# A rotation by 180 degrees: the last load in two transfers, and the first store issued only when the first of them has landed

## Chip, cores and metric

One core of a Trainium2 chip. The metric is device microseconds (us) of one execution; lower is better. Unless a line says otherwise, a time is the median of the runs of one session, and all runs compared here were at a granted clock of 1.0. A ratio is the mean time of one kernel's fast runs over that of the other's of the same rounds, so it is not quite the ratio of the medians beside it.

## The reference

```python
def setup_inputs():
    batch, c, h, w = 32, 3, 256, 256
    return {"x": np.random.randn(batch, c, h, w).astype(np.float32)}

def reference(x):
    return np.rot90(x, k=2, axes=(-2, -1)).astype(np.float32)
```

Each of the 96 images of 65,536 floats is reversed end to end: 25.17 MB in, 25.17 MB out.

## The kernel before

An image is cut into 4 rows of 16,384 floats, so 32 images fill 128 partitions of 64 KB each. Three tiles A, Bt and Ct hold all images. VectorE reverses each row in place, by swapping mirrored blocks of 2,048 floats through a scratch tile T; the store reverses the order of an image's 4 rows by its access pattern.

```python
    G = 32
    E = L // 4          # 16384
    J = E // 8          # 2048
    # ... views x4 (loads) and o4 (stores), tiles A, Bt, Ct, T: cut ...
    def load(t, g):
        nc.sync.dma_start(out=t[:, :], in_=x4[g])

    def store(t, g):
        nc.sync.dma_start(out=o4[g][:, ::-1, :], in_=t[:, :])

    def inside(t):      # 12 copies of 128 x 2048
        for lo in range(0, E // 2, J):
            hi = E - lo - J
            copy(T[:, :], back(t, hi, hi + J))
            copy(t[:, hi:hi + J], back(t, lo, lo + J))
            copy(t[:, lo:lo + J], T[:, :])

    load(A, 0)
    load(Bt, 1)
    load(Ct, 2)
    for g, t in enumerate((A, Bt, Ct)):
        inside(t)
        store(t, g)
```

All six transfers are issued by SP (SyncE) on one queue. So they pass through the 16 DMA engines in the order of issue: load A, load B, load C, store A, store B, store C.

## Time and profile before

| | before |
|---|---|
| median | 123.0 us (122.93 to 123.27, 3 runs) |
| span of the profiled run | 121.2 us |
| share of the span in which DMA engines hold packets | 97.4% |
| VectorE busy | 44.2 us, 36% |
| bytes moved | 50.33 MB |

The page, the timeline and the windows are read in the prediction below. One more view belongs to the argument: who waited for whom (columns: engine, line and tile that waited, what it waited for, us in total, times, longest).

```profile
DVE T L52 <- DMA Ct<-in_x_dram: 5.4, 1, 5.4
DVE T L52 <- DMA Bt<-in_x_dram: 4.3, 1, 4.3
```

VectorE does the same work on B and on C, and the loads are of equal size, but it waits 1.1 us longer for C. VectorE is not the bound, so that wait costs nothing by itself. It is a gauge: load C comes 1.1 us later than the rhythm of the loads would have it.

### The profile page before, as it was taken

What the parts mean: (1) busy time and instruction counts of PE and PEld (TensorE: products, weight loads), DVE (VectorE), ACT (ScalarE), POOL (GpSimd) and SP (SyncE); (2) the same over time, 40 slices, a digit from 0 to 9 for tenths busy, and PEclk for the clock granted to TensorE, in tenths of its full rate; (3) what the DMA queues carried; (4) which work ended last, traced back from release to release, by engine and by line L of the source; (5) the groups of instructions that cost most, each with busy time, mean ns of one, the idle gap of its engine ahead of it and who ended that gap; (6) DMA issues with size and microseconds to landing.
All of it is one profiled execution on the core that took longest, in us unless ns stands there. A gap on an engine that the chain in (4) does not pass through costs nothing.

```text
span 121.2 us, 91 instructions
## 1 busy us (share of the span) xinstructions
DVE 44.2 (36%) x36; POOL 0.2 (0%) x4
## 2 busy tenths in 40 slices
DVE  0000000599994199998039999500000000000000
POOL 0000000000000000000000000000000000000000
DMA  9779977997799879978989977997799779977980
GB/s 346 346 346 411 627 346 346 454 584 346 346 454 584 346 346 498 541 346 346 346 346 584 454 346 346 606 433 346 346 606 433 346 346 627 411 346 346 671 368 0
DMA packets 864, 50.33 MB, mean 415 GB/s; under 512 B 96, under 2 KB 96, under 8 KB 96
## 3 DMA queue, kind: packets, MB, share of 16 engines
q1 hardware_dynamic: 864, 50.33, 97.4%
HBM read 25.17 MB, written 25.17 MB: 415 GB/s over the span
## 4 chain that ended last, share of the span: by engine, by line
DMA 34%; DVE 25%; another core or an unknown queue 4%; issue 1%; SPq 0%; DVEq 0%
DMA Bt<-in_x_dram 34%; DVE T L52 8%; DVE Bt L52 8%; DVE Ct L52 8%; SPq L55 0%; DVEq L52 0%
## 5 line engine op out<-in xcount | busy, mean ns | idle before, releaser
L52 DVE COPY T<-A 128x2048 f32<-128x2048 f32 x4 | 4.9, 1227 | 22.7 <-DMA A<-in_x_dram 22.6
L52 DVE COPY T<-Ct 128x2048 f32<-128x2048 f32 x4 | 4.9, 1228 | 5.5 <-DMA Ct<-in_x_dram 5.4
L52 DVE COPY T<-Bt 128x2048 f32<-128x2048 f32 x4 | 4.9, 1227 | 4.4 <-DMA Bt<-in_x_dram 4.3
L52 DVE COPY A<-T 128x2048 f32<-128x2048 f32 x4 | 4.9, 1227 | 0.1
L52 DVE COPY Bt<-T 128x2048 f32<-128x2048 f32 x4 | 4.9, 1227 | 0.1
L52 DVE COPY Bt<-Bt 128x2048 f32<-128x2048 f32 x4 | 4.9, 1227 | 0.1
L52 DVE COPY Ct<-T 128x2048 f32<-128x2048 f32 x4 | 4.9, 1227 | 0.1
L52 DVE COPY A<-A 128x2048 f32<-128x2048 f32 x4 | 4.9, 1226 | 0.1
L52 DVE COPY Ct<-Ct 128x2048 f32<-128x2048 f32 x4 | 4.9, 1226 | 0.1
L87 POOL MEMSET const-bfloat16-1.0<- 128x1 bf16 x1 | 0.1, 102 | 0.0
L87 POOL MEMSET const-uint8-127<- 128x1 uint8 x1 | 0.1, 102 | 0.0
L87 POOL MEMSET const-float32-1.0<- 128x1 f32 x1 | 0.1, 99 | 0.0
L87 POOL MEMSET const-float32-0.0<- 128x1 f32 x1 | 0.1, 98 | 0.2 <-issue 0.2
## 6 DMA issues: line engine op xcount, KB each, us to landing
A<-in_x_dram SPq DMA_DIRECT2D x1, 21.8
Bt<-in_x_dram SPq DMA_DIRECT2D x1, 40.7
Ct<-in_x_dram SPq DMA_DIRECT2D x1, 60.7
out_dram<-A SPq DMA_DIRECT2D x1, 44.1
out_dram<-Bt SPq DMA_DIRECT2D x1, 44.0
out_dram<-Ct SPq DMA_DIRECT2D x1, 42.8
```

Source lines behind the costliest of these rows:

```text
L52: tc.keep_in_program_order(nc.vector.tensor_copy(out=dst, in_=src))
L87: nc = _bacc.Bacc("TRN2", target_bir_lowering=False, num_devices=1)
```

## The change

The intent is to keep the first store out of the DMA queue until the loads are nearly through, without paying for a wait with idle engines. The store is held back by a dependency (the *gate*) on most of the last load (the *body*, 58 KB of each row), and the remaining 6 KB of each row (the *tail*) keep the engines busy while the store is issued. The place where the queue goes over from loads to stores is called a *turn* below.

```diff
-    def load(t, g):
-        nc.sync.dma_start(out=t[:, :], in_=x4[g])
+    def load(t, g, lo, hi):
+        return nc.sync.dma_start(out=t[:, lo:hi], in_=x4[g][:, lo:hi])
 ...
-    load(A, 0)
-    load(Bt, 1)
-    load(Ct, 2)
-    for g, t in enumerate((A, Bt, Ct)):
+    TAIL = 1536
+    load(A, 0, 0, E)
+    load(Bt, 1, 0, E)
+    body = load(Ct, 2, 0, E - TAIL)
+    load(Ct, 2, E - TAIL, E)
+    inside(A)
+    first = store(A, 0)
+    tc.add_manual_dep(
+        first.ins, body.ins.name,
+        mybir.DependencyInfo(mybir.DependencyClass.Sync, mybir.DependencyReason.DATA),
+        reason="the first store is queued while the last strip is on its way")
+    for g, t in ((1, Bt), (2, Ct)):
         inside(t)
         store(t, g)
```

More of the change, by code (lines that the diff above doesn't have):

```diff
@@ L52, in copy @@
         tc.keep_in_program_order(nc.vector.tensor_copy(out=dst, in_=src))
-    def load(t, g):
-        nc.sync.dma_start(out=t[:, :], in_=x4[g])
+    def load(t, g, lo, hi):
+        return nc.sync.dma_start(out=t[:, lo:hi], in_=x4[g][:, lo:hi])
     def store(t, g):
-        nc.sync.dma_start(out=o4[g][:, ::-1, :], in_=t[:, :])
+        return nc.sync.dma_start(out=o4[g][:, ::-1, :], in_=t[:, :])
     def inside(t):
```

## The prediction

> **What bounds the kernel now.** I read the page first: the share of each engine, the DMA lines and the issues.
>
> ```profile
> DVE 44.2 (36%) x36; POOL 0.2 (0%) x4
> ...
> q1 hardware_dynamic: 864, 50.33, 97.4%
> HBM read 25.17 MB, written 25.17 MB: 415 GB/s over the span
> ...
> A<-in_x_dram SPq DMA_DIRECT2D x1, 21.8
> Bt<-in_x_dram SPq DMA_DIRECT2D x1, 40.7
> Ct<-in_x_dram SPq DMA_DIRECT2D x1, 60.7
> out_dram<-A SPq DMA_DIRECT2D x1, 44.1
> out_dram<-Bt SPq DMA_DIRECT2D x1, 44.0
> out_dram<-Ct SPq DMA_DIRECT2D x1, 42.8
> ```
>
> The 16 DMA engines hold packets during 97.4% of the span and VectorE works 36% of it, so the DMA engines are the bound, and the one VectorE chain matters only if a store is not queued when its turn comes. The last column of an issue is the time from issue to landing, most of which is standing in line behind the earlier transfers on the one queue.
>
> Next I asked the timeline when the transfers were issued, so that landings can be worked out.
>
> ```profile
> 0.73 0.39 SPq L55 DMA_DIRECT2D A<-in_x_dram  x1
> 1.18 0.42 SPq L55 DMA_DIRECT2D Bt<-in_x_dram  x1
> 1.64 0.43 SPq L55 DMA_DIRECT2D Ct<-in_x_dram  x1
> ...
> 37.70 0.63 SPq L58 DMA_DIRECT2D out_dram<-A  x1
> ...
> 57.11 0.55 SPq L58 DMA_DIRECT2D out_dram<-Bt  x1
> ...
> 77.58 0.54 SPq L58 DMA_DIRECT2D out_dram<-Ct  x1
> ```
>
> Issue plus time to landing gives landings at 22.5, 41.9, 62.3, 81.8, 101.1 and 120.4 us. The differences are 19.4, **20.4**, 19.5, 19.3 and 19.3: all transfers are equal in bytes, and one, the last load, takes about 1.1 us longer. Every store is queued long before its turn: A at 37.70 for 62, B at 57.11 for 82, C at 77.58 for 101. Then I looked at the moment in question, with windows as long as a packet (columns: stretch, its length, busy VectorE and GpSimd, clock, DMA share, GB/s).
>
> ```profile
> 55.60:58.00 2.40, 1.45 (x2) 0.00 (x0) 1.00 1.01 410
> 58.00:60.40 2.40, 0.00 (x0) 0.00 (x0) 1.00 1.29 382
> 60.40:62.80 2.40, 0.35 (x1) 0.00 (x0) 1.00 1.01 437
> 62.80:65.20 2.40, 2.33 (x3) 0.00 (x0) 1.00 1.01 437
> ```
>
> The rate dips and the packets' summed time rises (1.29 is more than all engines' time, because a packet is booked whole in the window where it starts). So packets that start at 58 to 60 are longer. The trace's records of single DMA packets say the same. Chained end to start, they give 16 engines of 48 packets of 65,536 bytes, 24 loads and then 24 stores:
>
> ```
> packet of each engine   starts (us)     ends (us)       length (us)   mean excess over 2.418
> 1st (first load)        1.74..2.40      4.84..5.30      2.63..3.46    0.72
> 2nd to 23rd                                             2.42..2.43    0.00
> 24th (last load)        57.98..58.44    61.42..62.06    3.17..3.86    1.13
> 25th (first store)      61.42..62.07    63.84..64.48    2.42          0.00
> 26th to 48th                            ..120.02        2.42          0.00
> ```
>
> The sum closes: a mean start of about 1.9, 48 x 2.418 = 116.1, 0.72 and 1.13 give 119.8, inside the spread of last ends, 119.38 to 120.02. **Apart from start and end, the only time not spent at line rate is 1.1 us where loads turn into stores.** That is all that this change can win.
>
> **What the Trainium skill says.** "DMA: Bandwidth & Descriptors", section "Where 436 GB/s comes from", puts the ceiling of the 16 ports at 435 GB/s. The trace agrees: 16 x 65,536 bytes in 2.418 us is 434 GB/s, the windows show 437, for loads and stores alike. Nothing is left inside the transfers. The same page, "Two DMAs through the same engine are not ordered", says that descriptors of one queue start in order but are pipelined, with separate queues for an engine's read and write sides. The trace fits: there is no gap between one load and the next, nor between stores. It follows, as my inference, that an engine can begin to read the first store's tile while the last load is still being written. The same page, "Latency and other measured facts", gives about 600 ns to the first byte for a transfer issued from SP. Here the first issue ends at 0.73 + 0.39 = 1.12 and the first packet starts at 1.74: 0.62, in agreement; the last of the engines starts 0.66 later. "SBUF — State Buffer", section "SBUF: two separate sides", says that compute and DMA do not share ports. Packets are 2.42 us with VectorE busy (at 30 us) and idle (at 90 us), so I give the 12 copies of 1.23 us per tile no part in this.
>
> **The change part by part.**
>
> (1) The last load is cut. Engine by engine, 8 packets of 65,536 bytes become 8 of 59,392 and 8 of 6,144. At the same bytes per us these are 2.418 x 58/64 = 2.191 and 0.227 us. The body takes 17.53 us from the start at 41.06 to 41.53, so its last data is there at 58.59 to 59.06; the tail would end 1.81 us later, at 60.40 to 60.87. One more issue of about 0.43 us falls near 2 us, where SP has nothing else to do: nothing on the path. Overhead of the eight small packets is not measured in this trace; I allow 0 to 0.3 us.
>
> (2) The first store waits. A landing is seen 0.32 to 0.37 us after an engine's last packet (22.21 to 22.57, 41.54 to 41.91, 62.07 to 62.39 in the records and VectorE's starts). SP may thus issue store A at 59.06 + 0.35 = 59.4 instead of 37.70. The issue takes 0.63 us, then 0.62 to the first packet: 60.65, and 0.66 more for the last engine, 61.3. The tail keeps the engines busy to 60.40 to 60.87, so they would idle some 0.3 us. Without the tail the wait would be naked, with 1.9 us of idleness; this is what the tail is for. Store B, ready at 57.08, now goes right after A, at about 60.1, still 20 us early.
>
> (3) What the 1.13 us becomes. It is inside the load's own last packet and delays the load's landing, while the first store shows nothing. I take it for the store's reads running into the last load. With no store in the ring, the tail should run at line rate. In return the first store starts cold and may have to fill, as the first load did (0.72 us mean excess; the last engine, which sets the end, only 0.22). I choose 0.2 to 0.6 for reading SBUF.
>
> Sum for the latest engine: the first store starts at 61.3, plus 0.4 of fill, against 62.07 today: -0.4 us. All later packets are 2.418 as before, so the end moves by the same amount.
>
> (4) VectorE waits for two landings of C instead of one, some hundredths of a us, and starts near 61.3 instead of 62.45. Store C is issued near 76.5 where it is needed at 100. Worth nothing either way.
>
> **The rivals.**
>
> *R1: the turn costs its 1.1 us whatever is queued*, for instance because reads from HBM must drain before the engine reads SBUF. For it: there is just one turn in the trace and it is the one slow place. Against it: the lateness lies in the load, not in the store. Then the tail's last packets stretch to 61.5 to 62.0, the store's late arrival at 60.65 to 61.3 hides in that, and the time stays at 122.9 to 123.2.
>
> *R2: the new wait costs more than it saves.* SP's wait for the body, issue and first packet is 1.9 us against a tail of 1.81, so any extra delay is idle time of all engines. If the store's fill is the first load's 0.72 and its issue is slow by another 0.5, the loss is 0.72 + 0.5 + 0.3 = 1.5 against 1.13 saved: 123.4.
>
> *R3: the whole 1.13 comes back*, because the store's descriptors arrive just in time and fill costs nothing: 122.0. For it: store packets show no excess anywhere. Against it: the arrival sum above is 0.3 us late before any fill.
>
> *R4: VectorE or a late store becomes the bound.* Against it: 20 us of slack for stores B and C, as worked out above. I give it nothing.
>
> **Range and chances.** The step from the median of 123.0 is my own mechanism's -0.4, so 122.6. R3 sets the favourable end, 122.0, and R2 the other, 123.4; the three runs of before span 0.34 us, so I widen slightly below: 121.9 to 123.4. To be faster by over 2% the change would have to win 2.46 us, more than twice what the turn costs; slower by over 2% needs 2.46 us of added idleness, a naked wait of 1.9 plus a full fill, with nothing won. I give each 0.01.
>
> **What would show each step.** In the changed trace the tail's landing minus B's landing shows the stretch: 19.4 us if it is gone, 20.4 if R1 holds. The issue of store A should stand at 59.4. Its landing minus the tail's landing shows idleness and fill: 19.3 plus 0.4 to 1.0. Store B and C should follow at 19.3 each. In the packet records, the eight small packets should last 0.23 us, with a gap of 0 to 0.6 us before the first store's packet, which is itself 2.4 to 3.0. The prediction would be wrong if the small packets were much dearer than their bytes, if the split load lost line rate all along its 58 KB packets, or if store packets written after the gate ran slower than 2.418.

## The result

The changed kernel takes 122.14 us (122.01 to 122.36, 5 runs) against 123.04 us (122.93 to 123.27, 5 runs): a ratio of 0.9928, 95% interval 0.9916 to 0.9941. That is 0.9 us, clear of noise and under 2%. The profiled spans went from 121.2 to 120.2 us.

The page of the changed kernel, DMA lines and issues (the last number of an issue is us to landing):

```profile
q1 hardware_dynamic: 1008, 50.33, 97.3%
HBM read 25.17 MB, written 25.17 MB: 419 GB/s over the span
...
Ct<-in_x_dram SPq DMA_DIRECT2D x1, 7424.0 KB, 57.7
Ct<-in_x_dram SPq DMA_DIRECT2D x1, 768.0 KB, 59.2
A<-in_x_dram SPq DMA_DIRECT2D x1, 21.8
Bt<-in_x_dram SPq DMA_DIRECT2D x1, 40.7
out_dram<-A SPq DMA_DIRECT2D x1, 21.3
```

The same bytes took 144 packets more (128 data packets of 6 KB and 16 for one more completion), and the rate over the span rose from 415 to 419 GB/s. Store A lands 21.3 us after its issue instead of 44.1. Its timeline and that of the other stores:

```profile
59.48 0.63 SPq L58 DMA_DIRECT2D out_dram<-A  x1
60.20 0.55 SPq L58 DMA_DIRECT2D out_dram<-Bt  x1
...
76.51 0.54 SPq L58 DMA_DIRECT2D out_dram<-Ct  x1
```

Store A went from 37.70 to 59.48, store C came 1.1 us earlier. The waits, against the two lines shown of before:

```profile
DVE T L52 <- DMA Ct<-in_x_dram: 4.4, 1, 4.4
DVE T L52 <- DMA Bt<-in_x_dram: 4.3, 1, 4.3
```

The gauge reads 0.1 us instead of 1.1: VectorE waits nearly as long for C as for B. So the slow place at the end of the loads is gone. The trace's records of single DMA packets, by the 16 engines, show it directly, with what came in its place (idle is the stretch of 57 to 64 us less the summed length of the packets in it):

```
                                before              after
last load data ends (us)        61.42..62.06        60.33..60.84
last 64 KB load packet          3.17..3.86          none (58 KB: 2.19, 6 KB: 0.23)
first store packet starts       61.42..62.07        60.76..60.94
first store packet, length      2.42                2.47..2.48
mean idle of an engine, 57..64  0.00                0.16
mean period of the packets of
  stores B and C                2.4147              2.4209
last store packet ends          119.38..120.02      118.90..119.11
```

The last engine now starts its stores 1.13 us earlier (60.94 for 62.07). It gives back 0.06 us in the first store packet and 0.0062 us in each of 24 store packets, which makes 0.15. The rest, 0.92, is the end's move from 120.02 to 119.11.

### The profile page after: what moved, and what is told of

Read it like the earlier page. It is cut to its first block, busy times and chain, and to the rows that moved or that the text cites. A ratio compares the mean times of both kernels' runs of the same rounds, so it can differ in the third digit from the quotient of the medians.

```text
span 120.2 us, 93 instructions
## 1 busy us (share of the span) xinstructions
DVE 44.2 (37%) x36; POOL 0.2 (0%) x4
## 4 chain that ended last, share of the span: by engine, by line
DMA 34%; DVE 25%; another core or an unknown queue 4%; issue 1%; SPq 0%; DVEq 0%
DMA Bt<-in_x_dram 34%; DVE T L52 8%; DVE Bt L52 8%; DVE Ct L52 8%; SPq L55 0%; DVEq L52 0%
## 6 DMA issues: line engine op xcount, KB each, us to landing
Ct<-in_x_dram SPq DMA_DIRECT2D x1, 7424.0 KB, 57.7
Ct<-in_x_dram SPq DMA_DIRECT2D x1, 768.0 KB, 59.2
out_dram<-A SPq DMA_DIRECT2D x1, 21.3
```

## The experiments

The theory: a store queued behind the last load is read ahead by the DMA engines, and this costs the load's last packets 1.1 us; the gate removes it and the tail hides the gate. The rivals: that the cutting of the load does it; that any turn from loads to stores costs as much; that the change of the written memory, not of the read one, costs it. Twelve runs tell these apart. All except the last gave the right result. What is said of packets comes from the one profiled run of each kernel; each time is compared with the kernel before in the same session. "In the ring" below is the issue's start plus 1.28 us, as measured from issue to first packet in the changed kernel (59.48 to 60.76).

### Only the cut, no gate

```diff
-    first = store(A, 0)
-    tc.add_manual_dep(first.ins, body.ins.name, ...)
+    store(A, 0)          # as early as before; the load stays cut in 58 + 6 KB
```

> The last load cut into 58 KB and 6 KB as in the change, but the first store issued as early as before (about 37.7 us). Theory (the store's reads, queued behind the load, run into the end of the load; the gate alone removes that): the tail lands about 20.4 us after B, the first store follows with no gap, 123.0 us. Rival (cutting the last load into small pieces is what removes the slow packet): tail lands 19.4 us after B and the time is near the changed kernel's 122.1 us.

Measured: 123.32 us against 122.99, ratio 1.0018 (1.0004 to 1.0031). The page's issues of this run:

```profile
Ct<-in_x_dram SPq DMA_DIRECT2D x1, 7424.0 KB, 58.0
Ct<-in_x_dram SPq DMA_DIRECT2D x1, 768.0 KB, 60.8
```

The tail is issued 0.47 us after the body in both kernels, so it lands 3.3 us after the body here, and only 2.0 us after it in the changed kernel (57.7 and 59.2). By the packet records, an engine's eight 6 KB packets take 3.13 us in the mean, 1.26 more than at the 0.234 of the changed kernel, and the excess is in the first five of them: the disturbance is whole, only spread over smaller packets. The cut without the gate is worth nothing; it costs 0.2%.

### Only a gate, no cut

```diff
     body = load(Ct, 2, 0, E)         # whole
     first = store(A, 0)              # depends on body
```

> The last load whole, the first store issued only when it has landed. Theory: the last load's packets all take 2.42 us (load C lands 19.4 us after B, near 61.2), then a naked wait: issue near 61.2, first store packet 1.25 us later, so engines idle 1.6 to 2.1 us; the store phase begins near 62.5, about 1.7 us later than in the changed kernel and 0.4 us later than before: 123.4 to 123.9 us. Rival (the turn from loads to stores costs 1.1 us by itself, whatever is queued): load C's last packets still take 3.5 us, and the time is above 124.5 us.

Measured: 122.52 us, ratio 0.9961 (0.9949 to 0.9973). This missed both expectations, and the reason was in the timeline: the scheduler let the second store, which had no such dependency, go first.

```profile
57.60 0.63 SPq L58 DMA_DIRECT2D out_dram<-Bt  x1
61.98 0.55 SPq L58 DMA_DIRECT2D out_dram<-A  x1
```

So this was not a naked wait. It became the first point of a series: a store in the ring at 58.9 us cost the last load packet 0.23 us on average, not 1.13. I repeated the run with both stores held back:

> The last load whole; both the first and the second store held back until it has landed, in the order A, B (in e2 the second store slipped ahead of the first at 57.6 us, so that run was not a naked wait). Theory: last load packets all 2.42 us, landing of C near 61.2, issue of store A near 61.2, first store packet 1.28 us after the issue, near 62.5: the store phase begins 1.4 us later than with timed gate 1 (60.9), 123.4 to 123.9 us. Rival (a turn costs 1.1 us of its own): the last load packets or the first store packet are 1 us longer, 124.5 us or more.

Measured: 123.92 us against 122.94, ratio 1.0074 (1.0041 to 1.0106). Windows of that run (stretch, its length, VectorE, GpSimd, clock, DMA share, GB/s) and its first issue:

```profile
58.00:60.40 2.40, 0.00 (x0) 0.00 (x0) 1.00 0.95 410
60.40:62.80 2.40, 1.40 (x2) 0.00 (x0) 1.00 1.03 437
62.80:65.20 2.40, 2.33 (x3) 0.00 (x0) 1.00 0.69 300
```

```profile
61.37 0.63 SPq L58 DMA_DIRECT2D out_dram<-A  x1
```

The share of over 1 in the stretch 58.0 to 60.4 of the kernel before is gone: all 24 load packets take 2.42 us (the third window's low rate is the hole seen through late booking, since a packet counts where it starts). The first store packet comes 1.27 us after the issue, at 62.64, and is 2.46 to 2.48 us long. The turn from loads to stores thus has next to no price of its own in this run (0.05 us in the first store packet); the engines just stand idle for 2.04 us on average. That is what the tail hides in the changed kernel, where 0.16 us of idleness are left. A gate without a tail loses.

### The moment of entry alone

Here the load is whole, and the store is held back by one or two extra VectorE copies after tile B's twelve, that is by time and not by a landing.

```diff
+    for _ in range(n):               # n = 1, 2
+        late = nc.vector.tensor_copy(out=T[:, :], in_=back(Bt, 0, J))
     first = store(A, 0)              # depends on the last of them
```

> The last load whole, and the first store held back not by a landing but by one extra VectorE copy after tile B's twelve (end near 58.3 us), so its packets should reach the engines near 59.6 us, 0.8 to 1.3 us before the last load packets would end at 60.4 to 60.9. Theory: part of the stretch comes back, last packets 2.4 to 3.6 us, time between 122.1 and 123.0. If the stretch needs only that a store is in the ring at any moment before the load's end, it is whole (3.55 us mean) and the time is 123.0. Rival (the split matters): 123.0 or more.

> As the run before with two extra VectorE copies (end near 59.6 us), so that store A is issued at the moment it is in the changed kernel, without any split of the load. Theory (the moment at which the store enters is all that counts): last load packets 2.42 us, first store packets near 60.9, 122.1 to 122.2 us, the same as the changed kernel. Rival (the split or the small packets do it): last packets 3.5 us and 123 us or more.

Measured: 122.0 us, ratio 0.9922 (0.991 to 0.9935), and 122.23 us, ratio 0.9941 (0.9929 to 0.9953). Both last load packets are undisturbed (means 2.436 and 2.439), and the time is that of the changed kernel without any cut. The second is as expected within noise; the first missed, for a part of the stretch was to come back: a store in the ring 0.7 to 1.2 us before the load's end does next to no harm (0.02 us). Its issue:

```profile
58.45 0.63 SPq L58 DMA_DIRECT2D out_dram<-A  x1
```

To find where the harm begins, the store was tied to the twelfth and to the eleventh copy of tile B itself:

```diff
+    first = store(A, 0)              # depends on copy number 12 (11) of inside(Bt)
```

> The last load whole, the first store held back until the twelfth and last copy of tile B (issue near 57.1, in the ring near 58.4, 2.0 to 2.5 us before the load's end without disturbance). e2, with a store in the ring at 58.9, showed 0.2 us of excess in the last load packet; timed gate 1, at 59.7, none. If the disturbance comes only when the store is there before the read side has finished the load, the excess here is between 0.2 and 0.8 us, 122.2 to 122.6 us. Rival (time in the ring does not matter once the store is there before the load's end): 1.1 us and 123.0.

> As the run before, held back until the eleventh copy of tile B (issue near 55.9, in the ring near 57.1, 3.3 to 3.8 us before the load's end, while the last but one packet of each engine is moved). If what counts is being there before the read side turns, the excess is whole, 0.9 to 1.2 us, 122.9 to 123.1 us. If the excess grows with the number of load packets that the store waits behind (as many as 9 in the kernel before), it is about 0.3 us and the time 122.3.

Measured: 122.3 us, ratio 0.9965 (0.9916 to 1.0013), and 123.06 us, ratio 1.0002 (0.9969 to 1.0035). The time of the first is not clear of noise (one of its four runs took 123.28), so the reading rests on its packets. The issue of the twelfth-copy run, then that of the eleventh-copy run with its window (to be held against 1.29 and 382 of before):

```profile
57.48 0.63 SPq L61 DMA_DIRECT2D out_dram<-A  x1
```

```profile
55.96 0.63 SPq L61 DMA_DIRECT2D out_dram<-A  x1
```

```profile
58.00:60.40 2.40, 0.00 (x0) 0.00 (x0) 1.00 1.18 355
```

Together, with mean excess of the last 64 KB load packet over 2.418 us:

```
first store in the ring at (us)   excess (us)   median time (us)
about 39    (before)              1.13          123.0
57.2        (eleventh copy)       1.10          123.06
58.8        (twelfth copy)        0.30          122.3
58.9        (store B slipped in)  0.23          122.52
59.7        (one extra copy)      0.02          122.0
60.9        (two extra copies)    0.02          122.23
62.65       (naked gate)          0.00          123.92
```

The times come from three sessions. It makes next to no difference whether the store stands in line for 22 us or for 4. The price falls from whole to a quarter between 57.2 and 58.8 us, while the last load packets start being recorded at 57.9 to 58.9. Past that, lateness brings idleness. I read it as the moment when an engine's read side has finished the loads; the trace has no record of the read side by itself, so this is an inference. Engine by engine it is not seen: in the twelfth-copy run the excess is 0.45 us for the packet that starts first, at 57.91, 0.73 for one at 58.32, 0.02 for one at 58.37 and 0.09 for the last, at 58.80.

### A longer tail

```diff
-    TAIL = 1536
+    TAIL = 2048
```

> The changed kernel with a tail of 2048 elements (8 KB of each row) instead of 1536. The body lands about 0.6 us earlier, so store A is issued near 58.85 and is in the ring near 60.1, 0.3 to 0.8 us before the tail's end. By timed gate 1 this is late enough for no disturbance and early enough for no idle time: the first store packets start right behind the tail, the time 121.9 to 122.1 us, 0.1 to 0.2 us under the changed kernel. If the disturbance starts as soon as the store is in the ring, up to 0.5 us slower instead.

Measured: 122.11 us, ratio 0.993 (0.9902 to 0.9959); issue at 59.08, mean idleness of an engine 0.035 us instead of 0.16. The tail is undisturbed. The tenth of a us that could be won is within noise of the changed kernel's 122.14: these two tails cannot be told apart, and others were not tried.

### How much store is needed for the harm

With timed gate 1 for the bulk, a strip of each row of tile A is stored early and waits behind the loads.

```diff
+    nc.sync.dma_start(out=o4[0][:, ::-1, :n], in_=A[:, :n])   # n = 128, 1024: early
     ...
+    first = nc.sync.dma_start(out=o4[0][:, ::-1, n:], in_=A[:, n:])   # depends on the extra copy
```

> As timed gate 1, but 512 bytes of each row of tile A (8 packets, 4 KB per engine) are stored early, queued behind the last load from about 37.8 us on, while the other 65,024 bytes of each row wait for the timed gate. If the lost 1.13 us is the store's reading ahead by bytes (at 27 bytes per ns it would be 31 KB per engine), 4 KB cost 0.15 us in the last load packet. If it is the price of any turn of the read side while loads are on the way, it is whole, about 1.1 us, in the last load packet. In both cases the gated rest follows at line rate; the time is 122.2 (bytes) or 123.1 us (any turn), plus some tenths for small packets.

> The same with 4 KB of each row early (8 packets, 32 KB per engine), the rest gated. Reading ahead by bytes: 32 KB are as much as the 31 KB above, so the whole 1.1 us. Any turn: also 1.1 us. With s1 this tells whether the cost grows with the bytes queued: s1 at 0.15 and this at 1.1 means bytes, both at 1.1 means the turn, both near 0 means that neither is right.

Measured: 122.01 us, ratio 0.9925 (0.991 to 0.9939), and 122.97 us, ratio 1.0002 (0.9986 to 1.0019). The last load packet's excess is 0.03 us with 4 KB per engine queued and 0.89 us with 32 KB, against 1.13 with the whole tile. (The strips were issued at 26.5 us, when the block they need was ready, not at 37.8; both are long before the moment that counts.) A turn to SBUF that is queued early is almost free when little follows, so the price is not for the turn; it grows with the bytes that are queued, from 4 KB to 32 KB by 0.86 us and from there to the whole tile by 0.24. At 27.1 bytes per ns (65,536 in 2.418 us), 0.89 us is the time of 24 thousand bytes and 1.13 us that of 31 thousand. The numbers were 0.15 and 1.1 in my sum, so bytes is the better theory, though not an exact one.

### Two turns in one program

```diff
     load(A), load(Bt)
-    load(Ct)
     store(A)
+    load(Ct)             # behind store A in the queue; then store(Bt), store(Ct)
```

Load C also depends on the last copy of tile A here, so that the scheduler leaves it behind store A; the stores have no gate.

> The same six transfers with the third load queued behind the first store: load A, load B, store A, load C, store B, store C, no gate anywhere. There are two turns from loads to stores and one from stores to loads. If each turn from loads to a queued store costs 1.1 us, the last packets of loads B and C take 3.5 us each, and the total is at least 1.1 us above the kernel before: 124.1 us if the turn from stores to loads is free, up to 125.2 if it costs as much. Rival (the loss is a single effect of the first store of the program, a cold start of the store path): load C's last packet is 2.42 us and the time is 123.0 to 123.3.

Measured: 122.92 us against 122.95, ratio 1.0005 (0.9982 to 1.0027). The windows around the two turns, load B to store A and load C to store B, and the issue of store B:

```profile
38.60:41.00 2.40, 0.00 (x0) 0.00 (x0) 1.00 1.42 437
...
77.80:80.20 2.40, 0.00 (x0) 0.00 (x0) 1.00 1.05 437
```

```profile
58.04 0.55 SPq L61 DMA_DIRECT2D out_dram<-Bt  x1
```

At the first turn the last load packet takes 3.29 to 3.48 us (mean excess 0.99), at the second 2.42 to 2.69 (mean 0.10), although store B had been in the queue for about 20 us. The turn from stores back to loads in between is clean, 2.418 on both sides. **My theory of a price at each such turn falls here; in this run, the only one with two turns, the price is paid once.** The rival, an effect of the first store of the program, was right in this, though not as a cold start of the store path: the naked gate's first store is just as cold and pays 0.05 us. What fits these runs is an inference: when the engines first come to a tile in SBUF with enough of it queued, their reading gains a lead over their writing of 24 to 31 thousand bytes, at the expense of the load that is still being written; a lead once gained is kept, so the second turn is nearly free. One small finding points the same way: in five runs where the store entered late (the changed kernel, both timed gates, the naked gate, the longer tail) the later store packets follow each other in 2.4205 to 2.4209 us, in all others in 2.4147 to 2.4151. But it does not follow the price: the run with 4 KB stored early, which paid 0.03 us, is at 2.4151, and the copy within HBM below, whose last load packet is clean, at 2.4147. No run here shows the lead itself.

### The written memory or the read one

In place of store A, a copy from HBM to HBM of the same size is queued behind the last load.

```diff
+    nc.sync.dma_start(out=o4[0][:, ::-1, :], in_=x4[0])
     inside(A)
-    store(A, 0)
```

> Wrong result on purpose: in place of the first store, a copy of the same size from HBM to HBM is queued right behind the last load (first third of the result comes out unreversed); then stores B and C. If the loss comes from the read side's change from HBM to SBUF, the 24th packet of each engine (last load) now takes 2.42 us, and the 1.1 us appear in the 32nd, the last of the HBM to HBM copy, just before store B begins to read SBUF. If it comes from the write side's change from SBUF to HBM, it stays in the 24th or 25th and the 32nd is clean. The copy's own packets may be slower than 2.42 us.

Measured: one run of 128.25 us, its state unknown, so that nothing is read from its time; the result is wrong, as intended (relative error 0.82). The window that was slow in the kernel before:

```profile
58.00:60.40 2.40, 0.00 (x0) 0.00 (x0) 1.00 0.95 410
```

The last load packet takes 2.426 us, with 64 KB packets that write HBM queued behind it since 2 us. So the change of the written memory from SBUF to HBM is not enough to cause it; in the runs here the price appears only where what follows reads from SBUF. No run has a transfer behind the load that reads SBUF without writing HBM, so it stays open whether reading from SBUF is enough alone. The second half of the expectation, 1.1 us in the 32nd packet, can't be judged: the copy's own packets, from the second on, take 2.76 to 4.25 us, and its last, at a mean of 3.51, does not stand out.

## Why the prediction was right, and where its sum was off

- **The bound and the size of the prize** held. The only slow place of the stream was the 1.13 us at the end of the loads, and no version's median got under 122.0 us. That the time fell inside the range says little, for the range ran from a gain of 1.1 us to a loss of 0.4; the forecast's own step, to 122.6, had less than half of the gain.
- **The mechanism of the gate** held: the small packets and 58 KB packets took 0.234 and 2.19 us (0.227 and 2.191 predicted), the body's data was there at 58.46 to 58.99 (58.59 to 59.06), SP issued store A at 59.48 (59.4), the first engine started it at 60.76 (60.65). Stores B and C had slack, VectorE's earlier start on C was worth nothing.
- **The step that was mis-sized is (3), with the end of (2)**: "the first store starts at 61.3, plus 0.4 of fill". Both numbers leaned on the program's first load. There the engines start over a spread of 0.66 us; store A's start over 0.18, so the last engine starts at 60.94 and not 61.3. And a cold store has next to no fill: 0.06 us, and 0.05 in the naked gate. Together 0.7 us better than the sum.
- **One cost was not in the sum**: the store packets follow each other 0.0062 us later than before, 0.15 us in all. The prediction had named store packets slower than 2.418 us as a sign of being wrong, and in this small measure it came: they are 2.424 long in the mean of stores B and C. The sum's -0.4 is -0.37 unrounded (61.3 + 0.4 - 62.07); corrected it is -0.37 - 0.36 - 0.34 + 0.15 = -0.92 us. The end of the packets moved by -0.91 and the median by -0.90.
- **Its other signs**: the tail lands 19.4 us after B, as foretold for a stretch that is gone, and store A 19.5 after the tail, where 19.7 to 20.3 was expected.
- **A reading of the windows was wrong**, without harm: a window of 2.40 us counts whole packets, so 437, 410 and 382 GB/s are 16, 15 and 14 packets of 65,536 bytes, and steps of one packet are no dip. The rate rests on the packet's length, 434 GB/s, and the slow place on the lengths and on the landings.
- **Rivals.** R1 (the turn costs its 1.1 us whatever is queued) is refuted by the naked gate, where no packet is long. R2 (the wait costs more than it saves) is what the naked gate does, at 123.92, but not the change. R3, all of it comes back, is nearest: 1.13 came back at the turn and 0.2 was given up again. R4 did not occur.
- **The cause** in step (3), "the store's reads running into the last load", has support from the series of entry times, from the strips and from the copy within HBM. It lacked a point: in the run with two turns it is no price of each turn but of the first one. That the reads are the means is not shown, for no trace here records them apart; why a store queued behind the load slows it while a copy from HBM does not, stays open.

## What to carry to other kernels

In a kernel bound by DMA, subtract landings of equal transfers from each other: a transfer that is late with nothing idle is worth a look at its packets; here it was 1.1 us that could be won. Issuing a store as early as possible isn't always free: here it was best to let it reach the queue in the last 1.2 us of the loads, by a dependency on all but a tail of the last load, with a tail as long as landing, issue and first packet take (about 1.9 us here); without the tail the same gate loses 1 us. The load need not be cut if the store can be held back by time, as the timed gates show. Here it was 0.7% of the time, and in the one run with two turns the second had only 0.10 us to win.

## What the Trainium skill lacked or had wrong

- "DMA: Bandwidth & Descriptors": no section tells that a store queued early behind loads can slow the load's last packets. Here 1.13 us per engine, 0.89 with only 32 KB per engine queued, 0.03 with 4 KB, 0.10 at the second such turn of a program, and 0.02 or less when the store enters in the last 1.2 us.
- "DMA: Bandwidth & Descriptors", section "Anatomy of one DMA — SWDGE (gpsimd) path", puts a fixed cost of about 2 us mostly on the receipt of the last write. It is written for transfers issued by GpSimd. For transfers issued by SP no page puts numbers on the way from one landing to the first packet of a transfer that depends on it, beyond the first byte that the prediction cites. The naked gate shows it: 2.04 us of idleness per engine in the mean; from the end of the last load packet of all (60.87) to the issue (61.37) 0.50 us, and from there to the first store packet (62.64) 1.27 us.
